# The input of a short convolution: seven products for eight pairs of 2 x 2 blocks in place of sixteen plain columns, and a shorter lookahead while their operands are made

## The chip, the cores and the metric

The kernel runs on one core of one Trainium2 chip. The metric is device time in microseconds of one execution. Three executions of the kernel before took 2119.58 to 2126.39 us, with a median of 2124.72 us.

The engines are named as the profile names them. PE is TensorE (matmuls), PEld its weight loads, DVE is VectorE, ACT is ScalarE, POOL is GpSimd and SP is SyncE, which here only issues DMAs. HBM is the memory off the core, SBUF the one on it, and PSUM the small memory that TensorE writes its sums into: eight banks of 128 x 512 words of 32 bits.

## The reference

One step of a four-layer decoder trunk is computed for a prompt of 512 tokens and for 8 samples of 4 tokens, 544 token columns in all, in float32. Each layer is a token mixer and a SwiGLU FFN, with a norm ahead of each. The mixers are pooling, a Conformer convolution, a chunked gating MLP and, in layer 3, the short convolution. Cut to what matters here:

```python
def _short_conv(h, buf, w_in, conv_w, w_out):
    L = h.shape[1]
    z = jnp.einsum('bld,de->ble', h, w_in)          # 1024 -> 3072
    bg, cg, xv = jnp.split(z, 3, axis=-1)
    cx = cg * xv
    ext = jnp.concatenate([buf.astype(cx.dtype), cx], axis=1)
    y = bg * _depthwise_causal(ext, conv_w)          # three taps a channel
    return jnp.einsum('ble,ed->bld', y, w_out), ext[:, L:]

def _swiglu(h, w_in, w_out):
    gate, up = jnp.split(jnp.einsum('bld,df->blf', h, w_in), 2, axis=-1)
    return jnp.einsum('blf,fd->bld', jax.nn.silu(gate) * up, w_out)
```

h is the input under an RMS norm; that is a gain for each channel and one factor r for each token. The last two rows of ext are an output as well, for the prompt and for the samples.

## The kernel before

**Layout.** Channels lie on the 128 partitions, in eight chunks, and tokens in the columns. The 544 tokens are kept as two halves, A (256 prompt tokens) and B (256 prompt tokens and the 32 sample tokens), named `_0` and `_1` in tiles.

**A float32 product from three.** TensorE multiplies in a reduced float32 format (fp32r). Each operand is split into a high part, a copy in that format, and a low part, which is the operand less its high part. A product is hi x hi + hi x lo + lo x hi. A weight block of 128 x 1024 is loaded as `raw` by SP (function `Load.dma`, L165); ACT makes `hi` (`Load.high`, L169); `lo` is made by DVE, by POOL, or by a "sum": ACT writes -hi (L176) and POOL issues a DMA that adds the weights from HBM to it (L177). One plain output column is 128 output channels for all tokens: 8 chunks x 3 parts x 2 halves, 48 matmuls of 256 and 288 columns.

**Seven products.** The FFN input of layers 2 and 3 has, beside plain columns, pairs (class `Pair`, function `seven`). A pair is a gate column and an up column, which is a matrix of 2 x 2 blocks: its two outputs by the two halves of the input channels (a11, a12, a21, a22). It is multiplied with 2 x 2 blocks of the input (the two halves of the channels by two token halves of 272 columns, b11 to b22) in Winograd's form of Strassen's algorithm. That takes seven products in place of eight, p1, p2, p5, p6, p7, p3, p4 in this order. Each is 4 chunks x 3 parts, 12 matmuls of 272 columns. Four of the seven left operands are sums of blocks (s1 to s4, tiles `ss`), made by DVE, and four right operands are sums t1 to t4. The results c11, c12, c21, c22 are put together by seven additions of DVE, by way of u2, u3 and u4. The low parts of a11, a12 and a22 are made by DMA sums (L248, L249), those of s1 to s4 by DVE.

The right operands need the norm's factor r, which is ready only some time after the norm's input. So the first columns of such an FFN are plain ones, which take r after the product (`LEAD`, four gate and four up columns), and a background job `operands` makes b11 to b22, t1 to t4 and their parts meanwhile, in four chunks. The fourth chunk reuses buffers and is made only when the last plain column has been written down (`st["led"]`, then `S.drain`).

**The order.** Every engine executes its queue in the order in which this Python program records it. `Stream.run` goes through the steps (a column or a product each): it first records the preparation of later operands (`fetch`: high parts up to four slots ahead, `AHI`, low parts up to three, `ALO`; a plain block is a slot, and two operands of a pair share one), then the step's matmuls, then the evacuation of the step before it. Background jobs are recorded in between, by a running estimate of each engine's time. At most four raw blocks are held (`NRAW`), and four sums (`NSS`).

**The short convolution before.** For each of the eight channel chunks c there are three plain columns: `sc` (cg), `sx` (xv) and, two at a time after every second chunk, `sbg` (bg). DVE makes all their low parts. Evacuation: cg times r squared (tile `st`), then the products with xv into the extended rows `se` (prompt) and `ss` (samples, with the state loaded by SP), three taps a chunk on DVE (`taps3`, tiles `sy`), and at bg the product with r, the product with the taps' result, and the split into high and low part for the output projection `so`. That reads eight chunks `sact[h][c]` for each of its columns.

Of the kernel before, what the change touches and what calls it, by code (L numbers as in the profile page):

```python
# [71 lines left out]
def trunk_kernel(  # L72
# [122 lines left out]
    class Pair:  # L195
# [3 lines left out]
        def __init__(self, src, name):  # L199
            self.name = name  # L200
# [13 lines left out]
    class Operand:  # L214
# [43 lines left out]
    class Stream:  # L258
        def __init__(self):
# [4 lines left out]
            self.held, self.fill = False, None  # L264

# [52 lines left out]
        def fetch(self, cur):  # L318
# [3 lines left out]
            def within(i, ahead):  # L322
                return i < len(self.loads) and self.loads[i].slot <= at + ahead
# [355 lines left out]
    def seven(pairs, st, out):  # L679
# [3 lines left out]
        def product(k, wt, name):  # L683
# [12 lines left out]
        def evac(pair, k, ps):  # L696
# [16 lines left out]
            else:  # L713
                out(pair, "c21", add(pair, "c21", ps, "u3"))
            yield

        for pair in pairs:
            for k, left, right in SEVEN:
                S.add([pair.ops[left]], lambda wt, p=pair, k=k, r=right: product(r, wt, f"{k}_{p.name}"),
                      lambda ps, p=pair, k=k: evac(p, k, ps), flush=(pair is pairs[0] and k == "p1"))  # L720

    def ffn(layer, n, nxt, halves=(0, 1), rel=False, fill=None, tail=0, free=False, phases=((0, HF), (HF, NF))):
# [5 lines left out]
        for pi, (j0, j1) in enumerate(phases):  # L728
# [63 lines left out]
            for j in lead:  # L792
# [10 lines left out]
                if joint and j == 0:  # L803
                    S.do(lambda: S.job(operands(n, st)))
            if joint:
# [3 lines left out]
                pairs = [Pair(w_fin[layer, j], f"w{layer}_{j}") for j in range(lead.stop, j1)]  # L809
                for j, p in zip(range(lead.stop, j1), pairs):  # L810
                    p.j = j
# [50 lines left out]
    def out_proj(src, acts, n, name, halves=(0, 1), rel=False, fill=None, between=None, pair=False):  # L862
# [8 lines left out]
        for q in range(NC // 2):  # L871
            ls = cols_of(src[q], f"{name}_{q}_{hn}", bool(rel))
# [561 lines left out]
    r2 = [None, None]  # L1434
    sext = [[None] * NC, [None] * NC]
    sexs = [None] * NC
    sconv = [[None] * NC, [None] * NC]
    sact = [[None] * NC, [None] * NC]
    sgate = {}
    LS3 = SB + DS  # L1440

    def cg_evac(ps, c):
        yield from n3.wait((A, B))
        for h in (A, B):
            w = HW[h]
            if c == 0:
                r2[h] = T(f"r2_{h}")
                dve.tensor_mul(r2[h][:, :w], n3.r[h][:, :w], n3.r[h][:, :w])
            t = sgate[h] = T(f"st_{h}_{c}")
            dve.tensor_mul(t[:, :w], ps[h][:, :w], r2[h][:, :w])  # L1450
        yield

    def xv_mm(wt, c):
# [4 lines left out]
        return mm(wt, n3.hs, (A, B), f"sx_{c}")  # L1458

    def cg_mm(wt, c):  # L1460
        for cc in ((0, 1) if c == 0 else (c + 1,)):
            if cc < NC:
                sexs[cc] = T(f"ss_{cc}")
                nc.sync.dma_start(sexs[cc][:, : DB * LS3], st_sc[cc])
        ps = mm(wt, n3.hs, (A, B), f"sc_{c}")
        return n3.first(ps, (A, B)) if c == 0 else ps

    def taps3(out, view, c):
        dve.tensor_scalar(out, view(0), col(C_SC + c), None, op0=ALU.mult)
        for k in range(1, SW):  # L1470
            dve.scalar_tensor_tensor(
                out, view(k), col(C_SC + k * NC + c), out, op0=ALU.mult, op1=ALU.add
            )

    def xv_evac(ps, c):
        yield from n3.wait((A, B))
        for h in (A, B):
            dve.tensor_mul(sext[h][c][:, SB : SB + HP], ps[h][:, :HP], sgate[h][:, :HP])
        w = HW[B]
        ev = b3(sexs[c][:, : DB * LS3])  # L1480
        dve.tensor_mul(ev[:, :, SB:], b3(ps[B][:, HP:w]), b3(sgate[B][:, HP:w]))
        pool.tensor_copy(sext[B][c][:, :SB], sext[A][c][:, HP : HP + SB])
        nc.sync.dma_start(o_sp[:, c, :], sext[B][c][:, HP : HP + SB])
        nc.sync.dma_start(o_ss[:, c], ev[:, :, DS:])
        yield
        for h in (A, B):
            y = sconv[h][c] = T(f"sy_{h}_{c}")
# [211 lines left out]
```

## Time and profile before

| | |
|---|---|
| median of three runs | 2124.72 us |
| lowest, highest | 2119.58, 2126.39 us |
| the profiled execution | 2125.66 us, span 2124.0 us, granted clock 0.998 |
| busy: PE, DVE, ACT, POOL | 2105.0, 1450.7, 1021.6, 617.9 us |
| bytes read from HBM | 318.00 MB |
| DMA queue of SP, share of the 16 engines | 44.3% |
| DMA queue of POOL, share of the 16 engines | 12.0% |

The span is the part of an execution that the profiler covers; the execution's own time is 1.66 us longer. Matmuls are pipelined and overlap each other's ends, so a matmul's own length (288 ns for 272 columns) is more than its share of the time. In a row of a group, xN is the number of instructions; in a row of the timeline the two first numbers are start and length, and what stands in square brackets is how long the engine sat idle before, and what it waited for. Buffer numbers are left out of the names in the profile, so `p_w` is any of the seven products of a pair, and `L_p` is the low part of an FFN product.

### The profile page before, as it was taken

The numbers are of one execution on the slowest core, as the hardware profiler recorded it, in microseconds if no ns is written. First come the engines' busy times: TensorE is split into PE (matmuls) and PEld (weight loads), VectorE is DVE, ScalarE is ACT, GpSimd is POOL, SyncE is SP. The second block draws the span as 40 slices with busy tenths as digits, with TensorE's granted clock in tenths as the row PEclk, the third lists the DMA queues.
The fourth block names the chain that finished last, engine by engine and source line by source line (L and its number), as shares of the span: only waits on it lengthen the run. The fifth ranks groups of instructions, "written<-read, shape, count | busy, mean of one in ns | idle before, by whom it ended". The sixth has DMA issues, their size and how long they took to land.

```text
span 2124.0 us, 42395 instructions
## 1 busy us (share of the span) xinstructions
PE 2105.0 (99%) x16700; PEld 2096.3 (99%) x16700; DVE 1450.7 (68%) x3186; ACT 1021.6 (48%) x1783; POOL 617.9 (29%) x482
## 2 busy tenths in 40 slices
PE   9999999999999999999999999999999999999998
PEld 9999999999999999999999999999999999999998
DVE  7767699623999566566287768586765649585776
ACT  5445543545444654444436546354521246363454
POOL 4010387879889840000023102011000001011120
PEclk9999999999999999999999999999999999999999
DMA  8545654545956465546545557466545455475562
GB/s 267 183 152 160 186 186 145 183 145 187 198 180 196 153 200 160 176 158 186 136 112 178 135 132 152 128 146 150 134 92 92 91 140 110 132 161 123 147 148 79
DMA packets 131056, 325.03 MB, mean 153 GB/s; under 512 B 32652, under 2 KB 39912, under 8 KB 130592
## 3 DMA queue, kind: packets, MB, share of 16 engines
q1 hardware_dynamic: 110376, 279.47, 44.3%
q0 software_dynamic: 19328, 41.53, 12.0%
q8 instruction: 132, 2.16, 0.4%
q10 hardware_dynamic: 1152, 1.32, 0.2%
q14 instruction: 68, 0.56, 0.1%
HBM read 318.00 MB, written 4.62 MB: 152 GB/s over the span
## 4 chain that ended last, share of the span: by engine, by line
PE 90%; DVE 6%; DMA 1%; ACT 1%; issue 1%; POOL 0%; DVEq 0%; ACTq 0%; POOLq 0%
PE ps_o L109 25%; PE p_w L109 18%; PE ps_g L109 13%; PE ps_u L109 12%; PE ps_gv L109 3%; PE ps_co L109 2%; PE ps_sx L109 2%; PE ps_sc L109 2%; PE ps_sbg L109 2%; PE ps_so L109 2%; PE ps_cg L109 2%; PE ps_ca L109 2%; DMA raw_fi<-in_w_fin 1%; PE ps_go L109 1%; DVE vT L109 1%
## 5 line engine op out<-in xcount | busy, mean ns | idle before, releaser
L109 PE MATMUL ps_o<-L_p,hi_fo 128*128 128x288 f32 (+1 forms) x1408 | 351.0, 288 | 0.1
L109 PE MATMUL ps_o<-H_p,hi_fo 128*128 128x288 f32 (+1 forms) x1408 | 350.8, 288 | 0.0
L109 PE MATMUL ps_o<-H_p,lo_fo 128*128 128x288 f32 (+1 forms) x1408 | 350.5, 288 | 0.0
L169 ACT CAST hi_fi<-raw_fi 128x1024 fp32r<-128x1024 f32 x192 | 200.9, 1048 | 126.6 <-DMA raw_fi<-in_w_fin 49.7
L109 PEld LDWEIGHTS ps_o<-L_p,hi_fo 128*128 128x128 f32 x1408 | 245.9, 188 | 1.2 <-DVE L_p L109 1.2
L109 PEld LDWEIGHTS ps_o<-H_p,hi_fo 128*128 128x128 f32 x1408 | 246.2, 188 | 0.2
L109 PEld LDWEIGHTS ps_o<-H_p,lo_fo 128*128 128x128 f32 x1408 | 246.2, 188 | 0.0
L169 ACT CAST hi_fo<-raw_fo 128x768 fp32r<-128x768 f32 (+1 forms) x192 | 149.4, 780 | 188.9 <-PE ps_o L109 107.5
L109 POOL TENSOR_TENSOR lo_fi<-raw_fi,hi_fi 128x1024 fp32r<-128x1024 f32 (+1 forms) x86 | 204.5, 2392 | 32.7 <-ACT hi_fi L169 9.8
L249 POOL DMA_DIRECT2D lo_w_a<-in_w_fin x92 | 79.4, 983 | 445.1 <-ACT lo_w_a L248 380.6
L109 DVE TENSOR_TENSOR lo_fo<-raw_fo,hi_fo 128x768 fp32r<-128x768 f32 (+1 forms) x128 | 113.5, 889 | 121.0 <-issue 66.6
L109 DVE SCALAR_TENSOR_TENSOR ct<-ce,colsT,ct 128x256 f32<-128x256 f32 x448 | 182.3, 481 | 0.0
L109 DVE TENSOR_TENSOR lo_fi<-raw_fi,hi_fi 128x1024 fp32r<-128x1024 f32 (+1 forms) x92 | 117.5, 1279 | 68.4 <-ACT t L749 17.0
L109 PE MATMUL ps_g<-hH_f,hi_fi 128*128 128x256 f32 (+1 forms) x464 | 124.8, 291 | 2.4 <-ACT hi_fi L169 2.4
L109 PE MATMUL ps_g<-hH_f,lo_fi 128*128 128x256 f32 (+1 forms) x464 | 124.2, 290 | 0.8 <-DVE lo_fi L109 0.8
L109 PE MATMUL p_w<-H_t_f,hi_w_s 128*128 128x272 f32 x432 | 124.4, 288 | 0.0
L109 PE MATMUL p_w<-L_t_f,hi_w_s 128*128 128x272 f32 x432 | 124.2, 288 | 0.0
L109 PE MATMUL p_w<-H_t_f,lo_w_s 128*128 128x272 f32 x432 | 124.2, 288 | 0.0
L109 PE MATMUL ps_g<-hL_f,hi_fi 128*128 128x256 f32 (+1 forms) x464 | 124.1, 290 | 0.0
L109 PE MATMUL ps_u<-hH_f,hi_fi 128*128 128x256 f32 (+1 forms) x464 | 124.0, 290 | 0.0
L109 PE MATMUL ps_u<-hL_f,hi_fi 128*128 128x256 f32 (+1 forms) x464 | 123.5, 289 | 0.0
L109 PE MATMUL ps_u<-hH_f,lo_fi 128*128 128x256 f32 (+1 forms) x464 | 123.2, 288 | 0.0
(428 smaller groups left out, 6608.1 us busy)
## 6 DMA issues: line engine op xcount, KB each, us to landing
raw_fi<-in_w_fin SPq DMA_DIRECT2D x192, 512.0 KB, 4.6
raw_fo<-in_w_fout SPq DMA_DIRECT2D x96, 384.0 KB, 3.2
raw_w<-in_w_fin SPq DMA_DIRECT2D x72, 512.0 KB, 4.3
raw_fo<-in_w_fout SPq DMA_DIRECT2D x96, 320.0 KB, 3.1
lo_w_a<-in_w_fin POOLq DMA_DIRECT2D x92, 256.0 KB, 5.0
raw_ci<-in_w_cin SPq DMA_DIRECT2D x32, 512.0 KB, 4.4
raw_co<-in_w_cout SPq DMA_DIRECT2D x16, 512.0 KB, 4.8
raw_gi<-in_w_gin SPq DMA_DIRECT2D x16, 512.0 KB, 5.1
```

Source lines behind the costliest of these rows:

```text
L109: return fn(*a, **k)
L169: act.copy(self.hi, self.raw)
L249: nc.gpsimd.dma_start(self.lo, self.pair.plain(self.k)[1], accum_op=ALU.add)
```

## The change

The weights of the short convolution's input are taken in another order: first the eight bg columns, plain, and then eight pairs (cg, xv) by seven products. The background job `operands` runs under the bg columns. The low parts of the bg columns are made by DMA sums, and so are, for these pairs, the low parts of five left operands: a11, a12, a22 from HBM as in the FFN, and s1, s2 from their tiles in SBUF. r is now in the right operands, so cg and xv need no factor.

A pair's evacuation: c11 and c12 are the cg, c21 and c22 the xv of the two token halves; their products go into `se` and `ss` when c12 and c21 are there. One step after c21 the taps are recorded, the first tap of each half on ACT (L1473 in the new file) and the others on DVE; in the step after that the product with bg, and the split.

A second edit holds the lookahead: while plain columns with a job for `operands` run, left operands of pairs are prepared only two slots ahead (`NEAR`), and after the drain four again. That also holds for the FFN of layers 2 and 3.

```diff
         def low(self):
             self.lo = self.half("lo", ALO + 1)
-            if self.k in SUMMED:
+            if self.k in self.pair.summed:
+                src = self.value(self.k) if self.k in self.sums else self.pair.plain(self.k)[1]
                 act.activation(self.lo, self.hi.bitcast(F32), AF.Copy, scale=-1.0)
-                nc.gpsimd.dma_start(self.lo, self.pair.plain(self.k)[1], accum_op=ALU.add)
+                nc.gpsimd.dma_start(self.lo, src, accum_op=ALU.add)
                 return
             dve.tensor_sub(self.lo, self.value(self.k), self.hi.bitcast(F32))
...
             def within(i, ahead):
+                if i < len(self.loads) and isinstance(self.loads[i], Operand):
+                    ahead = min(ahead, self.near)
                 return i < len(self.loads) and self.loads[i].slot <= at + ahead
...
                 if joint and j == 0:
                     S.do(lambda: S.job(operands(n, st)))
+                    S.do(lambda: setattr(S, "near", NEAR))
             if joint:
                 if pi == 0:
                     S.do(lambda: st.update(led=True))
                     S.do(S.drain)
+                    S.do(lambda: setattr(S, "near", AHI))
...
+    def taps3(out, view, c, first):
+        w = [col(C_SC + k * NC + c) for k in range(SW)]
+        if first is act:
+            act.activation(out, view(0), AF.Identity, scale=w[0])
+        else:
+            dve.tensor_scalar(out, view(0), w[0], None, op0=ALU.mult)
         for k in range(1, SW):
+            dve.scalar_tensor_tensor(out, view(k), w[k], out, op0=ALU.mult, op1=ALU.add)
...
+        if k == "c12":
+            dve.tensor_mul(e[B][:, SB + SX : SB + HP], s["c22"][:, :n], t[:, :n])
+            dve.tensor_mul(ev[:, :, SB:], b3(s["c22"][:, n:ST]), b3(t[:, n:ST]))
+        if k != "c21":
+            return
+        dve.tensor_mul(e[A][:, SB : SB + HP], t[:, :HP], s["c11"][:, :HP])
+        dve.tensor_mul(e[B][:, SB : SB + SX], t[:, HP:ST], s["c11"][:, HP:ST])
+        pool.tensor_copy(e[B][:, :SB], e[A][:, HP : HP + SB])
...
+    def sc_taps(c, e, ev):
+        ys = [T(f"sy_{h}_{c}") for h in (A, B)]
+        for h in (A, B):
+            taps3(ys[h][:, :HP], lambda k: e[h][:, k : k + HP], c, act)
+            if h == B:
+                taps3(b3(ys[B][:, HP:TW]), lambda k: ev[:, :, k : k + DS], c, dve)
+            yield
+        for h in (A, B):
+            y = ys[h][:, : HW[h]]
+            dve.tensor_mul(y, y, sgate[h][c][:, : HW[h]])
+            sact[h][c] = split(y, HW[h], f"sy_{h}_{c}")
+        yield
+        for h in (A, B):
+            split_lo(sact[h][c], ys[h][:, : HW[h]], HW[h], dve)
...
+    for q in range(NC // 2):
+        for i, l in enumerate(cols_of(w_sin[NC + q], f"sb{q}", 0, True)):
+            c = 2 * q + i
+            S.add([l], lambda wt, c=c: sc_mm(wt, c), lambda ps, c=c: bg_evac(ps, c), flush=(c == 0), fill=1)
+            if c == 0:
+                S.do(lambda: S.job(operands(n3, st3)))
+                S.do(lambda: setattr(S, "near", NEAR))
+    S.do(lambda: st3.update(led=True))
+    S.do(S.drain)
+    S.do(lambda: setattr(S, "near", AHI))
+    seven([Pair(w_sin[c], f"ws{c}", c, SUMMED + ("s1", "s2")) for c in range(NC)], st3, sc_out, sc_begin)
...
+NEAR = 2
 SUMMED = ("a11", "a12", "a22")
```

The queue of DVE from pair 2 to pair 3 of the new stage (`ws2` to `ws4` name the pair, 0 and 1 after `se` and `sy` the token half):

```order
L109 TENSOR_TENSOR c21_ws2_21384<-p4_ws2_21349,u3_ws2_21336 128x272
L109 TENSOR_TENSOR se_0_2_21196<-c21_ws2_21384,c11_ws2_21272 128x256
L109 TENSOR_TENSOR se_1_2_21198<-c21_ws2_21384,c11_ws2_21272 128x16
L109 TENSOR_TENSOR ss_ws4_s1_21398<-raw_ws4_1_21187 128x512
L109 TENSOR_TENSOR ss_ws4_s2_21402<-ss_ws4_s1_21398,raw_ws4_0_21040 128x512
L109 SCALAR_TENSOR_TENSOR sy_0_2_21418<-se_0_2_21196,colsT_74,sy_0_2_21418 128x256 x2
L109 SCALAR_TENSOR_TENSOR sy_1_2_21419<-se_1_2_21198,colsT_74,sy_1_2_21419 128x256 x2
L109 TENSOR_SCALAR sy_1_2_21419<-ss_2_21010,colsT_74 128x32
L109 SCALAR_TENSOR_TENSOR sy_1_2_21419<-ss_2_21010,colsT_74,sy_1_2_21419 128x32 x2
L109 TENSOR_TENSOR c11_ws3_21444<-p2_ws3_21405,p1_ws3_21423 128x272
```

Pair 2's taps stand behind the sums of pair 4 and ahead of pair 3's c11.

The queue of ACT at the same place:

```order
L243 CAST hi_ws4_s1_21400<-ss_ws4_s1_21398 128x512
L243 CAST hi_ws4_s1_21400<-ss_ws4_s2_21402 128x512
L1473 ACTIVATE sy_0_2_21418<-se_0_2_21196,colsT_74 128x256
L707 COPY p1_ws3_21423<-p1_ws3_21371 128x272
L1473 ACTIVATE sy_1_2_21419<-se_1_2_21198,colsT_74 128x256
L249 ACTIVATE lo_ws4_s1_21446<-hi_ws4_s1_21400 128x512 x2
L243 CAST hi_ws4_s3_21453<-ss_ws4_s3_21451 128x512
L243 CAST hi_ws4_s3_21453<-ss_ws4_s4_21455 128x512
L626 CAST H_sy_0_2_21472<-sy_0_2_21418 128x256
```

The first tap of pair 2, on which DVE's rows for `sy` depend, stands behind the high parts of the two sums of pair 4; in the kernel before, all taps are on DVE.

The queue of DVE in the FFN of layer 3, around the end of the plain columns (`w3_4` is the first pair, `_3_f3` the fourth chunk of operands), before:

```order
L109 TENSOR_TENSOR lo_w3_4_s3_23033<-ss_w3_4_s3_22952,hi_w3_4_s3_22954 128x512
L109 TENSOR_TENSOR lo_w3_4_s3_23033<-ss_w3_4_s4_22956,hi_w3_4_s3_22954 128x512
L109 TENSOR_TENSOR L_p_3_2_0_23015<-q_3_2_0_23009,H_p_3_2_0_23014 128x256
L109 TENSOR_TENSOR L_p_3_2_1_23019<-q_3_2_1_23011,H_p_3_2_1_23018 128x288
L109 TENSOR_TENSOR t_3_3_0_23091<-ps_g3_3_0_22959,r_f301_0_22547 128x256
```

and in the new program:

```order
L109 TENSOR_TENSOR L_b22_f3_3_23567<-b22_3_f3_23532,H_b22_f3_3_23566 128x272
L109 TENSOR_TENSOR ss_w3_4_s3_23572<-raw_w3_4_0_22908,raw_w3_4_1_22992 128x512
L109 TENSOR_TENSOR lo_w3_4_s3_23576<-ss_w3_4_s3_23572,hi_w3_4_s3_23574 128x512
L109 TENSOR_TENSOR ss_w3_4_s4_23578<-raw_w3_4_0_22908,ss_w3_4_s2_23464 128x512
L109 TENSOR_TENSOR lo_w3_4_s3_23576<-ss_w3_4_s4_23578,hi_w3_4_s3_23574 128x512
L109 TENSOR_TENSOR ss_w3_5_s1_23594<-raw_w3_5_1_23182 128x512
```

The sums s3 and s4 of the first pair and their low parts have moved from ahead of the fourth chunk to behind it, and each low part now follows its sum directly.

More of the change, by code (lines that the diff above doesn't have):

```diff
@@ L195, in trunk_kernel, with __init__ @@
     class Pair:
-        def __init__(self, src, name):
-            self.name = name
+        def __init__(self, src, name, j, summed):
+            self.name, self.j, self.summed = name, j, summed
             self.src = [src[:, i] for i in range(2)]
@@ L264, in __init__ @@
             self.held, self.fill = False, None
+            self.near = AHI
         def add(self, loads, mm, evac, flush=False, fill=None):
@@ L677, in operands, with seven, product @@
             yield 0.7
-    def seven(pairs, st, out):
-        def product(k, wt, name):
+    def seven(pairs, st, out, begin=None):
+        def product(p, left, k, wt, name):
+            if begin and left == "a11":
+                begin(p)
             ps = PS(name)
@@ L713, in evac @@
             else:
-                out(pair, "c21", add(pair, "c21", ps, "u3"))
+                more = out(pair, "c21", add(pair, "c21", ps, "u3"))
+                yield
+                yield from more or ()
+                return
             yield
@@ L718, in seven @@
             for k, left, right in SEVEN:
-                S.add([pair.ops[left]], lambda wt, p=pair, k=k, r=right: product(r, wt, f"{k}_{p.name}"),
+                S.add([pair.ops[left]], lambda wt, p=pair, k=k, l=left, r=right: product(p, l, r, wt, f"{k}_{p.name}"),
                       lambda ps, p=pair, k=k: evac(p, k, ps), flush=(pair is pairs[0] and k == "p1"))
@@ L808, in ffn @@
                     S.do(S.drain)
-                pairs = [Pair(w_fin[layer, j], f"w{layer}_{j}") for j in range(lead.stop, j1)]
-                for j, p in zip(range(lead.stop, j1), pairs):
-                    p.j = j
+                    S.do(lambda: setattr(S, "near", AHI))
+                pairs = [Pair(w_fin[layer, j], f"w{layer}_{j}", j, SUMMED) for j in range(lead.stop, j1)]
                 seven(pairs, st, lambda p, k, t, acts=acts, j0=j0: seven_out(p, k, t, acts, j0))
@@ L871, in out_proj @@
         for q in range(NC // 2):
-            ls = cols_of(src[q], f"{name}_{q}_{hn}", bool(rel))
+            ls = cols_of(src[q], f"{name}_{q}_{hn}", bool(rel), pair and q < 2)
             if pair and q == 0:
@@ L1445, in cg_evac, with sc_begin @@
             w = HW[h]
[L1446 to L1450, printed above, removed]
-        yield
-    def xv_mm(wt, c):
+            t = sgate[h][c] = T(f"sg_{h}_{c}")
+            dve.tensor_mul(t[:, :w], ps[h][:, :w], n3.r[h][:, :w])
+        yield
+    def sc_begin(pair):
+        c = pair.j
+        for cc in ((0, 1) if c == 0 else (c + 1,)):
+            if cc < NC:
+                sexs[cc] = T(f"ss_{cc}")
+                nc.sync.dma_start(sexs[cc][:, : DB * LS3], st_sc[cc])
         for h in (A, B):
@@ new lines, in sc_mm @@
+    def sc_mm(wt, c):
+        ps = mm(wt, n3.hs, (A, B), f"sbg_{c}")
+        return n3.first(ps, (A, B)) if c == 0 else ps
+    for q in range(NC // 2):
[5 more added lines that the diff above has]
+                S.do(lambda: setattr(S, "near", NEAR))
```

64 lines of the change are left out of this document (12 added, 52 removed).

## The prediction

> **What bounds the kernel now.** I read the page first, then the chain of waits in order of time, then the waits of single engines in the stages that the change touches. The page's first row says that TensorE leaves 19 us of the span unused.
>
> ```profile
> PE 2105.0 (99%) x16700; PEld 2096.3 (99%) x16700; DVE 1450.7 (68%) x3186; ACT 1021.6 (48%) x1783; POOL 617.9 (29%) x482
> ```
>
> The chain of waits (start, length, engine, tile, count) is nearly all TensorE. The edited stage begins with ps_sc at 1541.25 and ends where ps_so begins, at 1688.27: 147.02 us for 24 tiles of 48 matmuls at 6.02 us, and 2.5 us at its start. The p_w row is the seven-product work that two FFN layers already have: 35 products in 52.78 us, 1.508 us a product, 0.1257 us a matmul of 272 columns.
>
> ```profile
> 1374.90 52.78 PE p_w L109 x420
> ...
> 1541.25 6.02 PE ps_sc L109 x48
> ...
> 1688.27 48.10 PE ps_so L109 x384
> ```
>
> So fewer matmuls is time, as long as the other engines keep up. The question is VectorE (DVE), whose 68% is an average. The window below is two whole pairs of the old seven-product work (columns: length, busy time of PE, PEld, DVE, ACT, POOL, clock, DMA share, GB/s), then the waits of DVE in it, then its own instructions (start, length).
>
> ```profile
> 1301.14:1322.81 21.67, 21.67 (x175) 21.67 (x174) 18.64 (x41) 14.63 (x31) 5.17 (x6) 1.00 0.75 160
> ```
>
> ```profile
> DVE q_B L109 <- ACT c_w L775: 1.2, 2, 0.7
> DVE c_w L109 <- ACT p_w L700: 1.0, 1, 1.0
> DVE L_p L109 <- ACT H_p L622: 0.6, 2, 0.5
> ```
>
> ```profile
> 1301.14 0.68 DVE L109 TENSOR_TENSOR lo_w_a<-ss_w_s,hi_w_a 128x512 fp32r<-128x512 f32 x1
> ...
> 1302.95 0.43 DVE L109 TENSOR_TENSOR c_w<-p_w,p_w 128x272 f32<-128x272 f32 x1
> 1303.30 1.28 DVE L109 TENSOR_TENSOR lo_w_s<-ss_w_s,hi_w_s 128x512 fp32r<-128x512 f32 x2
> 1304.50 0.68 DVE L109 TENSOR_TENSOR ss_w_s<-raw_w,ss_w_s 128x512 f32<-128x512 f32 x1
> 1305.10 0.43 DVE L109 TENSOR_TENSOR u_w<-p_w,p_w 128x272 f32<-128x272 f32 x1
> 1305.57 0.79 DVE L109 TENSOR_TENSOR u_w<-p_w,u_w 128x272 f32<-128x272 f32 x2
> ...
> 1311.40 0.69 DVE L109 TENSOR_TENSOR ss_w_s<-ss_w_s,raw_w 128x512 f32<-128x512 f32 x1
> 1313.07 0.44 DVE L109 TENSOR_TENSOR c_w<-p_w,p_w 128x272 f32<-128x272 f32 x1 [0.97 <-ACT p_w L700]
> ...
> 1322.81 0.69 DVE L109 TENSOR_TENSOR lo_w_a<-ss_w_s,hi_w_a 128x512 fp32r<-128x512 f32 x1
> ```
>
> In these 21.67 us DVE never waits for TensorE: it is busy for 18.64 and waits 2.8 for ScalarE (ACT). The same instruction returns after 21.67 us, 10.83 us a pair, while TensorE needs 14 x 1.508 / 2 = 10.55. So **DVE is already the slower engine in this pattern**; it goes unseen because a phase has at most six pairs and TensorE may run several products ahead of it. The change puts eight pairs in a row, with more DVE work in each.
>
> **The change part by part.** All sums are against the profiled execution: span 2124.0, 2125.66 us with what lies around it, 0.94 above the median 2124.72.
>
> *TensorE.* Sixteen tiles x 6.02 = 96.3 us go; 56 products x 1.508 = 84.4 us come: -11.9 us. [...]
>
> *DVE, a pair.* Issue to issue, from the rows above: a 512-column instruction 0.60 us (1303.30 to 1304.50 is two), a 272-column one 0.35, or 0.47 where it needs the one before it (1305.10 to 1305.57). The convolution's prices stand in the old stage:
>
> ```profile
> 1575.51 1.01 DVE L109 SCALAR_TENSOR_TENSOR sy<-se,colsT,sy 128x256 f32<-128x256 f32 x2
> 1576.44 0.35 DVE L109 TENSOR_SCALAR sy<-se,colsT 128x256 f32<-128x256 f32 x1
> 1576.82 1.00 DVE L109 SCALAR_TENSOR_TENSOR sy<-se,colsT,sy 128x256 f32<-128x256 f32 x2
> 1577.74 0.23 DVE L109 TENSOR_SCALAR sy<-ss,colsT 128x32 f32<-128x32 f32 x1
> 1578.01 0.54 DVE L109 SCALAR_TENSOR_TENSOR sy<-ss,colsT,sy 128x32 f32<-128x32 f32 x2
> 1578.47 0.78 DVE L109 TENSOR_TENSOR sg<-ps_sbg,r_n 128x256 f32<-128x256 f32 x2
> 1579.17 0.79 DVE L109 TENSOR_TENSOR sg<-sg,sy 128x256 f32<-128x256 f32 x2
> ```
>
> Against an FFN pair of 10.83 us, two 512-column low parts go to DMA (-1.2) and the FFN's three gate products go (-0.8). The four products into the convolution's buffers come (about 0.9, estimated from the 272-column price by their 240, 32, 256 and 16 columns), two pairs of taps (2 x 0.92, since 1575.51 to 1576.44 is a pair), the sample taps (0.73, from 1577.74 to 1578.47) and the product with bg (0.70, from 1578.47 to 1579.17): 10.83 - 2.0 + 4.2 = **13.0 us a pair**, if the waits for ACT stay as long as the FFN's (1.4 us a pair). The order of the queues says that they do. ACT's rows show the first tap behind the two hi copies of sums that DVE has just issued: hi of s1 and s2 is the very pattern of the row at 1313.07, in which DVE lost 0.97 us; the new code meets it once a pair, and about 0.4 us more at L_sy or at the other tap. Bounds: no wait at all, 13.0 - 1.4 = 11.6 us a pair; twice the waits, 14.4. I take 13.0, the value that the nearest row gives.
>
> *The stage's end.* DVE's last anchor to TensorE is column bg 6, whose sums it can take up when TensorE starts bg 7, 6.0 us before the first product. From there to the last low part of sact[7] it has the fourth operand chunk (6.0 us: 1785.22 to 1791.22 below), four sg products (1.4), eight pairs at 11.6 without waits (92.8, less 1.3 for two sums done before), four w_sout low parts of 1024 columns (4 x 1.2, twice the 512 price), 8 x 1.4 of waits, and 1.5 at the opening where s3 and s4 each wait for their hi copy: 116.4 us. So it ends 110.4 us after the first product could start. TensorE would want sact[7] after 84.4 us of products and seven eighths of a 6.02 us column, at 89.7. The output projection's first column cannot pass its eighth chunk, so **20.7 us are lost there and in the products before, against 11.9 saved: +8.8 us**. With 11.6 us a pair it would be 11.2 + 1.5 less: -3.9.
>
> *The bg columns* keep their matmuls. Their low parts move from DVE to ACT and DMA, under 48 us of TensorE; the FFN's lead columns do just this with more DVE work, so this is taken at nothing. If that cover failed, one late low part would cost about the landing time of the DMA row below, 5.0 us, once.
>
> *The held lookahead in the two FFN layers.* Layer 3 (layer 2 reads alike):
>
> ```profile
> 1784.00:1810.00 26.00, 25.15 (x197) 24.50 (x196) 24.20 (x58) 16.17 (x35) 3.44 (x4) 1.00 0.50 109
> ```
>
> ```profile
> 1785.22 1.99 DVE L109 SCALAR_TENSOR_TENSOR b_f<-x,colsT,r_f 128x256 f32<-128x256 f32 x6
> ...
> 1791.22 0.69 DVE L109 TENSOR_TENSOR ss_w_s<-raw_w 128x512 f32<-128x512 f32 x1
> ...
> 1812.05 0.42 DVE L109 TENSOR_TENSOR L_p<-q_A,H_p 128x256 fp32r<-128x256 f32 x1
> ```
>
> ```profile
> 1809.59 36.15 PE ps_o L109 x288
> ```
>
> TensorE loses 0.85 us at the first product, waiting for the fourth chunk. The hold lets that chunk start some 1.4 us earlier (four 512-column instructions fewer ahead of it, 2.4 us, and about 1.0 of waits more), which ends the loss: -0.85. But DVE is busy for 24.20 of these 26 us, and the sums s3, s4 now follow the chunk, each with its low part directly behind it, waiting for ACT's hi copy, as s1 and s2 now do ahead of it: four times about 0.7 us (under the 0.97 of the row at 1313.07, which holds two copies), less some 0.5 of old waits that go, +2.3. The phase's last L_p ends at 1812.47; ps_o wants it at its sixth chunk, 1809.59 + 5 x 0.75 = 1813.3, so 0.9 is free. New loss 2.3 + 0.85 - 0.9, less the 0.85 gained: about +1.4 a layer. Bounds: -0.85 if the new waits close up, +2.3 if ps_o has no slack; I take +1.4, as the DVE of the first of these rows has none: **+2.8 us** for both.
>
> *DMA.* The four middle pairs (42.2 us from 1286.12) moved:
>
> ```profile
> q0 software_dynamic: 1728, 3.15, 48.1%
> q1 hardware_dynamic: 1083, 3.63, 28.3%
> ...
> lo_w_a<-in_w_fin POOLq DMA_DIRECT2D x10, 256.0 KB, 5.0
> ```
>
> A low part of 0.262 MB took 0.481 x 42.2 x 0.262 / 3.15 = 1.69 us of all engines, a weight half of 0.524 MB 0.283 x 42.2 x 0.524 / 3.63 = 1.73. A new pair needs 5 x 1.69 + 2 x 1.73 = 11.9 us, above TensorE's 10.55 but under DVE's 13.0. No row shows a sum whose source is SBUF; I take HBM's price, between half (10.2 a pair) and double (15.3). It lands in 5.0 us, and the program issues it six products ahead, 9 us at TensorE's pace, so the term adds nothing.
>
> Sum: 2125.66 + 8.8 + 2.8 = 2137.3, and 0.94 less for the median: **2136 us**.
>
> **The rivals.**
>
> 1. *TensorE stays the bound* (the faster side). DVE's lag is swallowed by the eight PSUM banks and the lookahead. For it: that is what happens in the FFN phases, with 10.83 against 10.55. Against it: there the lag grows 0.3 us a pair, here 2.4, and at the end nothing follows that does without sact[7]. It decides only from about 10.6 us a pair down, where 8 x 2.4 and the opening's 1.5 make up the 20.7. Time 2124.7 - 11.9 - 1.7 = 2111.
> 2. *DVE bounds, but the waits for ACT close up*, since ACT runs ahead once TensorE stalls: 2124.7 - 3.9, and -1.7 to +2.8 for the FFN layers: 2119 to 2124. For it: ACT is busy for 14.63 of 21.67. Against it: the waits are of ACT for DVE's own sums.
> 3. *Low parts land late.* Five sums a pair fill DMA to 92% at DVE's pace. If landing doubles to 10 us, the way from ACT through POOL and DMA to TensorE and back to DVE gets longer than seven products: 8 x 1.4 more, 2147; at double price for SBUF sources (15.3 a pair) 8 x 2.3 more, 2154. For it: a sum's buffer is free only when the DMA that reads it has landed, which ties DVE to DMA. Against it: 5.0 us is the landing at the rows' 76%.
>
> **How the numbers follow.** Forecast (2130 to 2142, with half the waits and with one and a half times) 0.55; rival 1 0.10; rival 2 0.26; rival 3 0.09. About 0.3%, 6.4 us, is what a measurement of this kernel can tell from no change: 2118.3 to 2131.1 counts as the same. The forecast gives 0.07 of its chance to that band and rival 2 gives 0.02 to the faster side: faster 0.12, same 0.31, slower 0.57. The range 2117 to 2146 leaves out most of rival 1 and the far end of rival 3.
>
> **What would show it.** In the profile after, over the seven products of ws: DVE busy above 85% with waits for ACT and few for PE; its period of two pairs near 26 us, against 21.67; TensorE's waits there on DVE (hi, lo of s sums, or PSUM) and one longer one at ps_so for L_sy or H_sy, together near 20 us. The first product of each FFN layer without its 0.85, and a wait of ps_o for L_p in its place. It is wrong if the products run at 10.55 us a pair to the end, if TensorE's waits name DMA, or if the two-pair period is under 24 us.

## The result and the profile after

The new program takes 2161.93 us (four runs, 2160.37 to 2163.84) against 2125.55 us for the kernel before (four runs). The ratio is 1.0169, with a 95% interval of 1.0152 to 1.0185: slower by 36 us, where 11 had been forecast and 2146 was the end of the range. The profiled execution took 2163.84 us, its span 2162.1 us, its mean granted clock 0.989 (0.998 before).

The chain of waits of the new program (start, length, engine or DMA, tile, count) names something that it does not name in this part of the kernel before, DMAs:

```profile
1538.29 5.98 PE ps_sbg L109 x48
...
1594.33 6.99 DMA lo_ws_a<-in_w_sin
1601.36 5.37 PE p_ws L109 x22
1611.14 13.50 DMA lo_ws_s<-ss_ws_s
1628.35 12.38 DMA lo_ws_a<-ss_ws_s
...
1667.39 11.02 DMA lo_ws_s<-ss_ws_s
...
1701.94 18.50 DMA raw_so<-in_w_sout
1725.91 44.85 PE ps_so L109 x341
1770.76 6.01 PE ps_g L109 x48
```

The same chain's first rows of ps_gv (999.82 before, 997.03 after), of the FFN's ps_g, of the edited stage and of the FFN behind it, taken from both kernels, give the table of where the 38.1 us between the two profiled spans lie:

| stretch | before | after | difference | forecast |
|---|---|---|---|---|
| all before the gating MLP of layer 2 | 999.82 | 997.03 | -2.8 | 0 |
| gating MLP of layer 2, from its first ps_gv | 166.33 | 162.63 | -3.7 | 0 |
| FFN of layer 2 | 375.10 | 378.63 | +3.5 | +1.4 |
| short convolution, input and output projection | 195.12 | 232.47 | +37.4 | +8.8 |
| FFN of layer 3 | 387.63 | 391.34 | +3.7 | +1.4 |

The first row is no effect: the change touches nothing there, and over the nineteen profiled executions of this study that stretch lies between 995.2 and 1005.3 us. The second is an effect, of an edit that the prediction had overlooked; it has a part of its own below.

TensorE's waits in the edited stage, from 1560 to 1740 (sum, times, longest), are nearly all for low parts that come by DMA; the kernel before has no wait of TensorE in its stage at all:

```profile
PE p_ws L109 <- DMA lo_ws_a<-in_w_sin: 15.7, 9, 3.7
PE p_ws L109 <- DMA lo_ws_s<-ss_ws_s: 10.9, 4, 5.0
PE ps_so L109 <- ACT H_sy L626: 3.1, 1, 3.1
PE p_ws L109 <- DMA lo_ws_a<-ss_ws_s: 0.7, 1, 0.7
```

They make 30.4 us. More goes where no wait is named. These are rows of TensorE's timeline around the first of them:

```profile
1597.94 0.28 PE L109 MATMUL p_ws<-L_t_n,hi_ws_a 128*128 128x272 f32 x1
1601.36 0.59 PE L109 MATMUL p_ws<-H_t_n,lo_ws_a 128*128 128x272 f32 x1 [3.13 <-DMA lo_ws_a<-in_w_sin]
1601.75 0.43 PE L109 MATMUL p_ws<-H_t_n,hi_ws_a 128*128 128x272 f32 x1
1601.98 0.43 PE L109 MATMUL p_ws<-L_t_n,hi_ws_a 128*128 128x272 f32 x1
...
1607.42 0.33 PE L109 MATMUL p_ws<-L_b_n,hi_ws_a 128*128 128x272 f32 x1
1607.58 0.29 PE L109 MATMUL p_ws<-H_b_n,lo_ws_a 128*128 128x272 f32 x1
```

Ahead of the wait and from 1607.58 on a matmul starts every 0.126 us, in between every 0.227, at a granted clock of 0.50. The 26 matmuls from 1601.36 to 1607.42 so cost 2.8 us more than they should. Over this stage, from the first product at 1588.78 to the end of the output projection, 169 matmuls stand further apart than that and take 18.7 us more than at 0.1257: some 140 of them, with 15 us, in stretches like this one, the others singly, the last matmul ahead of a wait or the first behind it. The two parts close the account: 672 matmuls at 0.1257 and the projection's 48.1 us are 132.6; with 30.4 of waits and 18.7 of slow matmuls 181.7, and 181.98 is what the stretch took.

The DMAs of this stage: the stage of the kernel before, then the part of the new one from its first product to 1726 (KB each, median us from issue to landing).

```profile
DMA packets 14024, 12.75 MB, mean 87 GB/s; under 512 B 11008, under 2 KB 11008, under 8 KB 14012
...
out<-ss SPq DMA_DIRECT2D x8, 8.0 KB, 9.5
```

```profile
DMA packets 18697, 20.31 MB, mean 148 GB/s; under 512 B 11520, under 2 KB 11520, under 8 KB 18688
...
raw_ws<-in_w_sin SPq DMA_DIRECT2D x12, 512.0 KB, 11.1
lo_ws_a<-in_w_sin POOLq DMA_DIRECT2D x18, 256.0 KB, 11.0
...
lo_ws_s<-ss_ws_s POOLq DMA_DIRECT2D x10, 256.0 KB, 10.6
...
out<-ss SPq DMA_DIRECT2D x8, 8.0 KB, 15.0
```

A low part lands after 11 us, where the FFN's had 5.0. VectorE waits for these sums too, since only four sums of blocks are held and one is free only when the DMA that reads it has landed (sum, times, longest, in the new program from 1600 to 1715):

```profile
DVE ss_ws_s L109 <- DMA lo_ws_s<-ss_ws_s: 10.6, 4, 5.5
```

Both stages hold some 11000 packets under 512 B. The `out<-ss` rows are most of them: each sends two words for each of 8 samples and 128 channels, 1024 packets of 8 bytes. The next fence shows what one of them does: when SP issues the first, and the rate in GB/s of the 40 slices of 0.75 us from 1600 on.

```profile
1603.56 0.43 SPq L1494 DMA_DIRECT2D out<-ss  x1
```

```profile
GB/s 199 197 213 202 205 298 279 333 350 329 263 221 77 165 41 22 14 16 8 16 8 11 8 5 35 107 137 175 240 270 309 306 306 303 289 263 214 188 96 32
```

From the 15th slice on, 1610.5, the rate lies between 5 and 41 GB/s for 8 us, with sums in flight all the while. The 13.50 us of the chain's row at 1611.14 are a sum that went out into this.

### The profile page after: what moved, and what is told of

Same layout as the page of the kernel before. It is cut to its first block, busy times and chain, and to the rows that moved or that the text cites. A ratio compares the mean times of both kernels' runs of the same rounds, so it can differ in the third digit from the quotient of the medians.

```text
span 2162.1 us, 42598 instructions
## 1 busy us (share of the span) xinstructions
PE 2110.8 (98%) x16604; PEld 2099.0 (97%) x16604; DVE 1482.3 (69%) x3308; ACT 1092.5 (51%) x1927; POOL 654.9 (30%) x530
## 4 chain that ended last, share of the span: by engine, by line
PE 88%; DMA 6%; DVE 4%; ACT 1%; issue 1%; POOL 0%; DVEq 0%; SPq 0%; ACTq 0%; POOLq 0%
PE ps_o L109 24%; PE p_w L109 17%; PE ps_g L109 13%; PE ps_u L109 12%; PE ps_gv L109 4%; PE ps_go L109 2%; PE ps_co L109 2%; PE ps_sbg L109 2%; PE ps_so L109 2%; PE ps_cg L109 2%; PE ps_ca L109 2%; DMA lo_ws_s<-ss_ws_s 2%; PE ps_gu L109 1%; DMA lo_ws_a<-ss_ws_s 1%; DMA raw_so<-in_w_sout 1%
## 5 line engine op out<-in xcount | busy, mean ns | idle before, releaser
L243 ACT CAST hi_w_s<-ss_w_s 128x512 fp32r<-128x512 f32 x128 | 77.4, 622 | 93.0 <-DVE ss_w_s L109 90.7
```

Of the source, the lines that this page charges most:

```text
L243: act.copy(self.hi, self.value(k))
```

## The experiments

Four theories stood against each other, named by letters in what was expected. **V**, the prediction's: VectorE bounds the stage with some 13 us a pair. **D**: the DMA engines are full or held up by the small packets, and the low parts are late. **L**: a low part takes its 10 us by its own path through ACT, POOL and DMA, whatever else is moved. **H**: the held lookahead costs the FFN layers more than was priced, by late DMA sums.

All results, with the ratio to the kernel before (run beside it) and its 95% interval, and the length of the stage (short convolution's input and output projection) in the profiled execution. Three programs have the very stage of the new program, with 232.5, 233.2 and 237.6 us, so that with the packets in it a difference of 5 us in that column says little:

| run | median us | ratio | stage us |
|---|---|---|---|
| kernel before | 2125.55 | 1 | 195.1 |
| new program | 2161.93 | 1.0169 (1.0152 to 1.0185) | 232.5 |
| one write of the samples' rows | 2141.89 | 1.0079 (1.0061 to 1.0097) | 209.6 |
| same, packets of 64 bytes | 2140.51 | 1.0071 (1.0046 to 1.0097) | 207.2 |
| kernel before, one write | 2124.38 | 0.9990 (0.9980 to 0.9999) | 195.1 |
| two taps less | 2168.17 | 1.0204 (1.0187 to 1.0221) | 229.6 |
| one write, two taps less | 2127.06 | 1.0008 (0.9992 to 1.0024) | 191.9 |
| s1, s2 by VectorE | 2163.39 | 1.0187 (1.0172 to 1.0202) | 227.2 |
| s1, s2 by VectorE, two taps less | 2154.23 | 1.0131 (1.0112 to 1.0150) | 218.5 |
| one write, s1, s2 by VectorE | 2147.55 | 1.0098 (1.0079 to 1.0118) | 214.0 |
| one write, s1, s2 by POOL | 2159.69 | 1.0161 (1.0135 to 1.0187) | 224.2 |
| same, no hold in the FFN | 2149.26 | 1.0108 (1.0079 to 1.0138) | 223.4 |
| no hold in the FFN | 2153.96 | 1.0145 (1.0115 to 1.0174) | 233.2 |
| one write, no hold anywhere | 2131.91 | 1.0025 (1.0015 to 1.0036) | 203.9 |
| same, early first taps | 2123.94 | 0.9981 (0.9971 to 0.9991) | 199.0 |
| same, output columns paired, sums | 2126.25 | 0.9998 (0.9984 to 1.0013) | 201.3 |
| same, output columns paired, no sums | 2117.67 | 0.9966 (0.9951 to 0.9982) | 192.9 |
| kernel before, gating MLP's edit alone | 2122.71 | 0.9980 (0.9970 to 0.9990) | 195.2 |
| new program without that edit | 2176.36 | 1.0229 (1.0211 to 1.0247) | 237.6 |

### The small packets

One write of the samples' rows, after the last chunk, in place of eight:

```diff
-        nc.sync.dma_start(o_ss[:, c], ev[:, :, DS:])
+        pool.tensor_copy(sso[:, c], ev[:, :, DS:])
+        if c == NC - 1:
+            nc.sync.dma_start(o_ss, sso)
```

> The new program with one edit: the samples' last two rows, which go out as 1024 packets of 8 bytes for each channel chunk, are copied by POOL into one tile and leave in a single DMA after the last chunk. Theory D (the 16 DMA engines are full in the pairs, and the sums land late because of it): in the old stage the queue of SP took 47.2% of 147.02 us, 69.4 us, of which 24 weight halves at 1.73 us make 41.5; 27.9 us are then left for 11008 packets under 512 B, and 8192 of them go here, 20.8 us. D expects about 2142 us (2136 to 2150), with landings of sums near 7 us in place of 11. Theory V (VectorE bounds, as the prediction had it): 2162, unchanged. Theory L (a sum takes its 10 us whatever else the DMA engines do, because ACT, POOL and DMA follow one another): 2157 to 2162.

2141.89 us, and in the stretch from 1595 to 1700 the sums land in half the time:

```profile
DMA packets 9941, 19.19 MB, mean 183 GB/s; under 512 B 3021, under 2 KB 3021, under 8 KB 9933
...
lo_ws_a<-in_w_sin POOLq DMA_DIRECT2D x18, 256.0 KB, 5.8
...
lo_ws_s<-ss_ws_s POOLq DMA_DIRECT2D x10, 256.0 KB, 6.2
```

So D holds and L falls: the landing time is not the path's own. Whether it is the packets, or SP's queue standing at these DMAs until VectorE has written the rows, the next run tells, in which the eight DMAs stay:

```diff
+        pool.tensor_copy(sso[:, c], ev[:, :, DS:])
-        nc.sync.dma_start(o_ss[:, c], ev[:, :, DS:])
+        nc.sync.dma_start(o_ss[:, c], sso[:, c])
```

> As the run with one write of the samples' last rows, but they still leave in eight DMAs, one a channel chunk, at the same place in SP's queue; POOL has copied them side by side, so that a DMA has 128 packets of 64 bytes in place of 1024 of 8. Same bytes, same number of DMAs, same waits of SP. If the number of packets is what delays the sums: 2142 (2139 to 2147). If it was SP's queue, which stands at these DMAs until VectorE has written the rows: near 2162.

2140.51: the number of packets it is. And in the kernel before, with the one write in place of its eight:

> The kernel before, with the samples' last rows sent out in one DMA as in the runs above. There too each of the eight DMAs of 1024 packets takes 8.5 us to land, but no wait of TensorE names a DMA in that stage. If the packets cost only what waits behind them: no change, 2120 to 2127. If they cost time of their own: some 15 to 20 us faster, as in the new program.

2124.38, at 0.9990 of the kernel before, and the stage takes the same 195.1 us. The packets occupy the DMA engines there too: from 1545 to 1685 they are busy for 0.47 of the time with the packets and for 0.28 without, at 87 and 89 GB/s. But TensorE waits for no transfer in that stage, so the same packets cost it nothing. They became dear by what the change put beside them.

### VectorE

The second and third tap are left out (so the short convolution is not computed in full), with the packets and without:

```diff
         for k in range(1, SW):
-            dve.scalar_tensor_tensor(out, view(k), w[k], out, op0=ALU.mult, op1=ALU.add)
+            pass
```

> The new program without the second and third tap of the short convolution (the first tap alone is computed; it leaves out part of the computation). VectorE loses 4 instructions of 0.49 us and 2 of 0.25 a pair, 2.5 us a pair, 20 us in all; DMA keeps all it had. Theory V: 2142 to 2146. Theory D: 2158 to 2162, since DMA still has the same work. Theory L: 2158 to 2162.

> The one write, and without the second and third tap (it leaves out part of the computation): VectorE 2.5 us a pair less, DMA unchanged. Theory V: VectorE's 13.0 us a pair become 10.5, TensorE's pace, so nearly all that the stage loses goes: 2118 to 2126. Theory D: the waits for the sums with a source in SBUF stay, 2136 to 2142; at most the wait of ps_so for H_sy, 3.6 us, goes.

With the packets 20 us of VectorE's work are worth nothing: 2168 against 2162. That is above all three ranges, and why it is 6 us slower stays open. Without the packets they are worth 14.8 us, and the stage 17.7. So both theories are right, one behind the other. How well V's price was, VectorE's timeline shows by one instruction that comes once a pair, at a distance of two pairs; the new program, then the one with the one write:

```profile
1630.98 0.24 DVE L109 TENSOR_SCALAR sy<-ss,colsT 128x32 f32<-128x32 f32 x1
...
1663.56 0.23 DVE L109 TENSOR_SCALAR sy<-ss,colsT 128x32 f32<-128x32 f32 x1
```

```profile
1631.03 0.24 DVE L109 TENSOR_SCALAR sy<-ss,colsT 128x32 f32<-128x32 f32 x1
...
1657.22 0.23 DVE L109 TENSOR_SCALAR sy<-ss,colsT 128x32 f32<-128x32 f32 x1
```

32.6 us for two pairs with the packets, 26.19 without, where the prediction had 26.

### The sums s1 and s2

Their low parts by VectorE, as in the FFN:

```diff
-    seven([Pair(w_sin[c], f"ws{c}", c, SUMMED + ("s1", "s2")) for c in range(NC)], ...)
+    seven([Pair(w_sin[c], f"ws{c}", c, SUMMED) for c in range(NC)], ...)
```

> The new program with the low parts of s1 and s2 made by VectorE, as in the FFN, in place of DMA sums with a source in SBUF. DMA loses 16 sums of 1.93 us (69.4 us of the POOL queue over 36 sums), 31 us; VectorE gets 1.2 us a pair more, 9.6 us. Theory D: faster than the new program, 2140 to 2150, where VectorE's 14.2 us a pair becomes the next bound (the prediction's 2137 and 9.6 more). Theory V: slower, about 2171. Theory L: the longest path of a sum, from DVE's s1 through ACT, POOL and DMA, goes, so 2140 to 2155 too; D and L are told apart by the run before this one.

2163.39, outside what any theory had: 31 us of DMA work less bought nothing. Two further runs asked why, the same without two taps, and the same with the one write:

> The packets of 8 bytes as in the new program, s1 and s2 low parts by VectorE, and without the second and third tap (it leaves out part of the computation). VectorE has 11.7 us a pair where the run with s1 and s2 by VectorE had 14.2. If VectorE had become the bound there, so that the 31 us of DMA work could not show: 2143 to 2152. If each burst of packets sets the pace whatever the amount of the other DMA work: within 4 us of that run, 2159 to 2166.

> The one write, and s1 and s2 low parts by VectorE: DMA 31 us less than the one write alone, VectorE 9.6 us more. If VectorE is what bounds once the packets are gone: 2149 to 2154 (2141.9 and 9.6). If what is left there is the lateness of the sums with a source in SBUF, which go: 2128 to 2138.

The first gave 2154.23, between its two forecasts. Set against the run without taps alone (2168.17), taking these sums off DMA is worth 14 us when VectorE has time, and nothing when it has not. The second gave 2147.55: without packets the sums are better on DMA, by 5.7 us. Its two pairs on VectorE take 28.60 us, 14.3 a pair, where 13.0 + 1.2 had been expected:

```profile
1638.38 0.23 DVE L109 TENSOR_SCALAR sy<-ss,colsT 128x32 f32<-128x32 f32 x1
...
1666.98 0.23 DVE L109 TENSOR_SCALAR sy<-ss,colsT 128x32 f32<-128x32 f32 x1
```

With the packets, then, the two limits lie close together: an edit that lifts one of them alone (two taps less, or two sums less) shows nothing that counts, both together shorten the stage by 14.0 us, and only the packets' own removal frees 22.9. How the bursts divide between filling the DMA engines and holding up what is in flight, these runs don't separate; that the sums from HBM still land after 11.2 us with s1 and s2 taken off DMA (11.0 in the new program) speaks for the second.

The low parts of s1 and s2 by POOL, with the one write:

```diff
-            dve.tensor_sub(self.lo, self.value(self.k), self.hi.bitcast(F32))
+            eng = pool if self.k in self.pair.pooled else dve
+            eng.tensor_sub(self.lo, self.value(self.k), self.hi.bitcast(F32))
```

> The one write, and the low parts of s1 and s2 made by POOL from SBUF in place of ACT and DMA sums. The run with the one write still waits 9.5 us for sums whose source is SBUF, and its TensorE then runs at 0.227 us a matmul for some 6 us after each of the three waits. If these sums are what is left (theory D): 10 to 16 us faster than the one write alone, 2126 to 2132. If VectorE is what bounds now, as the prediction had it (theory V): 2140 to 2144, since VectorE's work is the same.

2159.69, 18 us slower than without that edit, where neither theory had a loss. VectorE's timeline, then POOL's, at the same place:

```profile
1641.55 4.29 DVE L109 SCALAR_TENSOR_TENSOR sy<-se,colsT,sy 128x256 f32<-128x256 f32 x4 [1.10 <-ACT sy L1475]
...
1657.17 3.50 DVE L109 TENSOR_TENSOR ss_ws_s<-raw_ws,raw_ws 128x512 f32<-128x512 f32 x1
```

```profile
1640.95 3.16 POOL L109 TENSOR_TENSOR lo_ws_s<-ss_ws_s,hi_ws_s 128x512 fp32r<-128x512 f32 x2
...
1657.27 1.60 POOL L109 TENSOR_TENSOR lo_ws_a<-ss_ws_s,hi_ws_a 128x512 fp32r<-128x512 f32 x1
1658.52 1.59 POOL L109 TENSOR_TENSOR lo_ws_s<-ss_ws_s,hi_ws_s 128x512 fp32r<-128x512 f32 x1
```

Four taps that take 1.92 us in the run with the one write take 4.29, and a sum that takes 0.68 there takes 3.50, just while POOL subtracts. VectorE, which bounds here, loses that time: its two pairs take 31.38 us (1631.32 to 1662.70, the instruction used above), where the run with the one write has 26.19. This is V again, by a road that was not foreseen. The same with the FFN layers freed of the hold:

> The one write, s1 and s2 by POOL, and no hold in the FFN layers. The hold cost 3.3 and about 4 us by the traces, so 7 us faster than the same without that edit: 2119 to 2125 by theory D, 2133 to 2137 by theory V; kernel before is at 2123 to 2125.

2149.26: the stage is as slow as before (223.4 us), and the two FFN layers give back 9.5 us in the trace, 10.4 in the medians.

### The hold

The FFN layers without the held lookahead:

```diff
                 if joint and j == 0:
                     S.do(lambda: S.job(operands(n, st)))
-                    S.do(lambda: setattr(S, "near", NEAR))
```

> The new program without the held lookahead in the two FFN layers (it stays in the short convolution). Theory H (the hold makes the first pair's DMA sums late: 3.3 us of wait for lo_w_a in each layer, 375.1 to 378.6 us for layer 2 and 387.6 to 391.3 for layer 3): 7 us faster than the new program, about 2155, and the wait for lo_w_a gone. The prediction's price for the hold (DVE's s3 and s4 late, 2.8 us in all): 2159. If the hold is no cost there: 2162.

2153.96, 8 us faster than the new program (its four runs lie between 2149.45 and 2161.90); the two layers are back at 375.36 and 387.18 us. Over all profiled executions, layer 2 takes 380.2 us with the hold (mean of 10) and 375.2 without (9), layer 3 391.7 and 387.8: 8.9 us for both. What the hold did is seen in POOL's queue around layer 3's first product, which starts at 1786.73 before and at 1821.39 after:

```profile
1769.92 1.73 POOL L249 DMA_DIRECT2D lo_w_a<-in_w_fin  x2 [4.71 <-ACT lo_w_a L248]
1791.53 1.73 POOL L249 DMA_DIRECT2D lo_w_a<-in_w_fin  x2 [19.87 <-ACT lo_w_a L248]
```

```profile
1811.07 0.86 POOL L250 DMA_DIRECT2D lo_w_a<-in_w_fin  x1 [0.34 <-ACT H_p L626]
1829.00 0.85 POOL L250 DMA_DIRECT2D lo_w_a<-in_w_fin  x1 [17.07 <-ACT lo_w_a L249]
```

The sum for a22, which the pair's last product needs, went out 4.8 us after the first product before (the first of the two at 1791.53), and 7.6 us after it now, waiting for ACT. It lands 5 us later, at 1834.0. TensorE gets there earlier:

```profile
1834.07 0.59 PE L109 MATMUL p_w<-H_t_f,lo_w_a 128*128 128x272 f32 x1 [3.31 <-DMA lo_w_a<-in_w_fin]
```

No hold anywhere, with the one write:

> The new program with the one write and with the full lookahead everywhere, in the short convolution too. FFN layers: 7 us less than the one write alone. Short convolution: its first pair waits 3.35 us for lo_ws_a, with 1.7 us of slow matmuls behind it; without the hold this should go, as in the FFN, against 0.85 for the fourth chunk: 4 us less. 2131 (2127 to 2136). If the hold is needed there: 2135 to 2140.

2131.91, and of the first pair's wait for a low part from HBM 0.4 us are left. The hold was of no use in any of the three places.

### An edit that the prediction overlooked

The change has a third edit. In the gating MLP of layer 2 the low parts of the first four output columns of half A are no longer subtracts of POOL but DMA sums:

```diff
-            ls = cols_of(src[q], f"{name}_{q}_{hn}", bool(rel))
+            ls = cols_of(src[q], f"{name}_{q}_{hn}", bool(rel), pair and q < 2)
```

The kernel before shows what these subtracts did: a row of POOL, one of VectorE at the same time (vT takes 0.48 elsewhere), and a wait of TensorE for a later vT, up to which VectorE's queue has no gap. TensorE waits 2.6 us in this stretch, and not at all in the new program's.

```profile
1093.57 2.40 POOL L109 TENSOR_TENSOR lo_go<-raw_go,hi_go 128x1024 fp32r<-128x1024 f32 x1 [5.43 <-ACT hi_go L169]
```

```profile
1093.72 2.53 DVE L109 SCALAR_TENSOR_TENSOR vT<-vT,mv,lng 128x256 f32<-128x256 f32 x1
```

```profile
1102.29 1.27 PE L109 MATMUL mix<-gk,vT 128*128 128x128 f32 x8 [2.19 <-DVE vT L109]
```

The edit alone in the kernel before, and the new program without it:

> The kernel before with one edit of the change that the prediction had passed over: in the gating MLP of layer 2, the low parts of the first four output columns of half A are DMA sums in place of POOL subtracts. In the traces the stretch from that stage's first ps_gv to the FFN of layer 2 takes 166.3 and 169.1 us in the two kernels without this edit and 162.6 in the fourteen with it and one 163.3. Beside POOL's subtracts VectorE's vT takes 2.5 us in place of 0.5, and TensorE waits 2.2 us for it. If that edit makes the difference: 3.5 to 6.5 us faster than the kernel before, stretch 162.6. If the stretch is short for another reason: no change.

> The new program without that edit: 3.5 to 6.5 us slower than the new program, 2165 to 2168, stretch 166 to 169; else 2162.

2122.71, 3 us faster, a little less than the 3.5 to 6.5 expected, and the stretch is 162.63 us: the edit makes it. The new program without it takes 2176.36 and that stretch 167.07 us, 4.4 more. Of the other 10 us 5.2 lie in the edited stage (237.6), 3.0 in the two FFN layers and the rest ahead of the gating MLP; the code is the same there, and I have no cause for them.

### A version that beats both

From here each edit goes on top of the last. First the two first taps (ACT) directly behind the product that they read, one step ahead of VectorE's taps:

```diff
+        for h in (A, B):
+            act.activation(ys[h][:, :HP], e[h][:, :HP], AF.Identity, scale=col(C_SC + c))
         return sc_taps(c, e, ev, ys)
```

> As the run before, and the first taps of both halves (ACT) are recorded directly behind the product that they read, one step ahead of VectorE's taps. In the run with the one write VectorE waited 9.4 us for them, 10 times. Theory V (VectorE bounds once the packets are gone): 5 to 9 us faster than the run before, about 2123. If VectorE doesn't bound, or ACT's waiting at its queue's head delays the high parts as much: within 3 us of it.

2123.94. VectorE's two pairs now take 23.82 us (1612.88 to 1636.70, the same instruction). Then the output projection's first two columns side by side, chunk by chunk, with the low parts of four columns as DMA sums:

```diff
-    out_proj(w_sout, sact, nf3, "so")
+    out_proj(w_sout, sact, nf3, "so", pair=True)
```

> As the run before, and the output projection starts with two columns side by side, chunk by chunk, so that the last chunk is wanted one column later, and the low parts of its first four columns are DMA sums: VectorE has 4 x 1.2 us less. Theory V: the wait of ps_so for H_sy, 3.6 us, and the slow matmuls behind it, 2.7 us, go: 4 to 8 us faster than the run before, 2115 to 2119. If those sums are late as others were: within 3 us of it.

2126.25, a miss: the wait for H_sy is gone, but TensorE now waits 4.8 us in the projection for these sums. The same with the low parts left to VectorE:

> The run with the early first taps, and the output projection starting with two columns side by side; low parts of w_sout stay with VectorE (in the run before this edit with DMA sums they were 4.8 us late). The wait of ps_so for H_sy, 3.4 us, and 2.5 us of slow matmuls behind it should go: 2118 to 2121. If VectorE's low parts are late for two columns at once: 2124 to 2128.

2117.67, 0.9966 of the kernel before (0.9951 to 0.9982) and 44 us faster than the new program. Of what it gains on the kernel before, 3.7 us come from the gating MLP's edit and 2.2 from the stage. TensorE's waits from 1530 to 1760, and the projection in the chain without a gap:

```profile
PE p_ws L109 <- DMA lo_ws_s<-ss_ws_s: 6.3, 4, 3.7
```

```profile
1680.86 48.04 PE ps_so L109 x384
```

Of the 11.9 us that TensorE saves in the stage, 6.3 still go into waits and 3.5 into slow matmuls. Putting some bg columns between the pairs, to give VectorE time, was not tried: their inputs would have to be kept while the operands need the room.

## Why the prediction was wrong

**TensorE, -11.9 us: right.** In the run with one write and two taps less the stage takes 191.85; less its 5.7 us of waits and 2.9 of slow matmuls that is 183.2, and 195.12 - 11.9 is 183.2.

**VectorE, 13.0 us a pair: right, but in the new program it was not the bound.** 13.1 without the packets, 14.3 with s1 and s2 added, and 1.2 less with ACT's first tap out of the way. The waits for ACT, which the prediction took at 1.4 us a pair from the FFN, add up to 11.9 us in the run with the one write (1600 to 1700), about 1.5 a pair. In the new program itself VectorE waits for DMA as well, 13.2 us from 1600 to 1715, and its two pairs take 32.6 us.

**DMA, "so the term adds nothing": this step failed.** The working added five sums and two weight halves, 11.9 us a pair, and took 5.0 us for a landing, from FFN rows. It left out what else moves in the short convolution: the view of DMAs of the old stage has `out<-ss` with 9.5 us to land and 11008 packets under 512 B, and was read for neither. The FFN rows that gave the 5.0 us hold 320 packets under 512 B among 2815, and their landing time did not carry over. The price is 232.47 - 209.58 = 22.9 us, 2.9 a pair. Rival 3 had the landing (10 us) and the name of TensorE's wait, but took it from the sums' own load, at 1.4 us a pair and a chance of 0.09. The sign given for a wrong forecast, "if TensorE's waits name DMA", is what came.

**The loss at the end, 20.7 us: mis-sized.** With the packets gone it is 16.5 of waits and 9.7 of slow matmuls, 26.2. Of the waits 3.3 are the first pair's, for a sum that the hold makes late, which was not forecast for this stage; the others are for the sums of s1 and s2 (9.5) and for H_sy (3.6). That they come from VectorE's pace, as forecast, is shown by the run with two taps less, in which 5.7 us of waits are left. The slow matmuls were not in the sum: after some of the waits a matmul starts every 0.227 us in place of 0.126, at a granted clock of 0.50 (1601.36 to 1607.40 in the new program). In the new program's stage those stretches make 15 of the 18.7 us.

**The bg columns at nothing: right.** From 1538.29 to 1588.78 are 50.5 us; eight columns of 6.02 and 2.5 at the start are 50.7.

**The gating MLP: not in the sum.** -3.7 us, from an edit in the diff that the prediction's parts do not list. Its rows stood in the trace of before, and they would have shown, too, how VectorE fares beside POOL's subtracts (vT takes 2.53 us in place of 0.48).

**The FFN layers, +2.8 us: wrong mechanism, size 8.9.** The first product's wait did shrink, as forecast (0.2 us is left in layer 2, none in layer 3). But the hold delays not only VectorE's sums s3 and s4 but the first pair's sums by DMA too, and it is a22 that is late, by 3.3 us in each layer. No wait of ps_o for L_p is seen.

## What to carry to other kernels

Before a transfer that an engine waits for is put into a stage, list what else is in flight there with its packet count and its landing time: here 64 KB in packets of 8 bytes cost nothing in the kernel before, where nobody waits for a transfer (without them the time is 0.9990 of that with them), and 22.9 us in the stage of the new program, where TensorE does. Two bounds that lie close together hid each other here, so an edit that lifted one alone showed little, and one had to lift both to see either. A wait of TensorE should be priced with the slow matmuls that follow it: here 15 us of them beside 30.4 us of waits.

## What the runs showed of the hardware

**Packets of 8 bytes.** Behind the DMA of 1024 of them that SP issues at 1603.56, the transfer rate lies between 5 and 41 GB/s for 8 us, and in the new program's stage, with eight such DMAs, the 256 KB sums from HBM land in 11.0 us in place of 5.8 with one write. With the same bytes in 128 packets of 64 the program takes 2140.51 us, as with one write (2141.89).

**The clock after a wait.** Two waits of the same length in the two FFN layers of the new program ended differently, by the windows behind them (stretch, length, busy times of PE, PEld, DVE, ACT, POOL, granted clock, DMA share, GB/s):

```profile
1223.60:1229.00 5.40, 4.95 (x37) 4.73 (x38) 4.83 (x12) 3.69 (x7) 0.86 (x1) 1.00 0.79 163
...
1834.07:1839.60 5.53, 5.53 (x24) 5.53 (x25) 4.96 (x12) 3.70 (x7) 0.86 (x1) 0.50 0.77 170
```

Both waits were 3.31 us; behind the first the clock stays at 1.00, behind the second it is 0.50 for 5.5 us, 24 matmuls in place of some 44. So the length of a wait alone does not tell what follows it. In the new program's edited stage matmuls at 0.227 us follow waits of 3.13 us (up to 1601.36) and of 0.96 (up to 1622.36, at a clock of 0.50 again), and none follow waits of 3.19 (up to 1619.57) and 2.70 (up to 1660.26). Between the waits of 3.19 and 0.96 lie 1.8 us of matmuls. The slow stretches there that no other wait breaks last 4.0 to 6.1 us. What decides whether a wait costs was not shown.

**VectorE beside POOL's subtract.** With its tensor operands in SBUF, VectorE's vT takes 2.53 us beside one subtract of POOL where 0.48 is usual, 2.0 more (kernel before, above), and the sum of two raw blocks 3.50 beside two where 0.68 is usual, 2.8 more (one write, s1 and s2 by POOL). Instructions with one operand in PSUM did not take longer: in the kernel before, two of `gt<-ps_gv,r_n` take 0.78 us at 1113.54, beside a subtract of POOL from 1112.14 to 1114.55, and 0.78 at 1090.50, beside none.
